# Reciprocal roots on GpSimd, gate steps on ScalarE, and fixed places for weight splits and the compression block in a two-layer hybrid trunk

## The chip, the cores and the metric

One core of one Trainium2 chip. The metric is the device time of the kernel in microseconds, one launch; of several runs the median is given.

## The reference

Two layers over one sequence of 256 tokens, width 1024, all in fp32. `D` is the width, `gate` a sigmoid of a small projection; the attention part is told in words.

```
for l in range(2):
    proj = rms_norm(h, norm_mix[l]) @ w_in[l]
    hq, hf, hi, hg, nq, kc, vc, ksl, vsl, ksw, vsw, ngate = split(proj)
    # HGRN2, 4 heads of 128, chunks of 64
    f = lb + (1 - lb) * sigmoid(hf);  k = 1 - f;  q = silu(hq)
    o_hg = rms_norm(gated_linear_recurrence(q, k, hi, log f)) * silu(hg)
    # NSA, 8 query heads of 64, 2 key/value heads
    kc, vc = compress(kc, ...), compress(vc, ...)   # silu(flat @ w1) @ w2
    o_nsa = gate * (compressed, selected and sliding-window attention),
            with q and all k normed (rms over 64) and rotated
    h = h + concat(o_hg, o_nsa) @ w_out[l]
    g, u = split(rms_norm(h, norm_ffn[l]) @ w_ffn_in[l])
    h = h + (silu(g) * u) @ w_ffn_out[l]
```

## The kernel before

Each fp32 product is made of three matmuls in a reduced format: `mm3` (L318 to L322) multiplies high parts with high parts, and each high part with the other low part. So each weight tile is split. Weights come in units of 128x1024 fp32 (512 KB): a DMA on the sync queue brings `wraw` (L122, four buffers), ScalarE copies it into the rounded `whi` (L142), and VectorE subtracts, `wlo = wraw - whi` (L143). Units are split five ahead of use, and six split units are held. Activations are split in the same way (`x`, L346 and L347).

The order on each engine is made by a scheduler from priorities; `after(a, b)` puts `a` behind `b` in that order without a semaphore of its own, and `products` is the list of all matmuls that `mm3` has issued, by which such places are named.

A layer runs: the norm and its transposition (`norm_T`, L324), the token projections B, C and A (`pt`), of which A gives the queries (`sq`, `qk_ss`, `qn`); the root `qk_rs` of the mean squares of queries and keys (`rstd`, L260 to L274); the gates of two heads (`gates(0)`, L376: `pf` for `hf`, `pq` for `hq`, two units each, 48 matmuls each); the compression block: `phid` (L505, 64 records, with the eight `w1` loads of 512 KB of L465), its copy `hid`, `phT` (L511), the SiLU (`hsg`, `hk`, `hv`), `pkc` (L522, L525), the compressed keys' root `kc_rs` and `kcb` (L544), `pkT` (L546). Then the scaled keys (`kraw`, L555, and `kA`, `kB`) and queries (`qn`, L570, and `qA`), `gates(1)`, the scores `pS`, the attention outputs, the recurrence (`pd`, `pl`, `po`, with the root `h_rs`), the output projection (`py`), the residual (L858), the feed-forward's norm with `norm_T`, the first feed-forward block by token tiles (`pgt`, `pgT`), and the feed-forward loop (`pgu`, `pz`).

`rstd` makes the reciprocal root on VectorE: a shift trick and three Newton steps, twelve operations. It is called four times in a layer: `qk_rs` (128x24), `kc_rs` (32x1) and `h_rs` (128x4, twice). `norm_T` makes its root already on GpSimd, by `pow` (L334, L335).

Around the feed-forward's norm the splits have places: the `wlo` of the first two feed-forward units stand behind the `x` subtractions of token tile 0, if they are made by then, and the `whi` of the next unit behind the last `x` copy:

```python
        last, lo = norm_T(0, gain1, *X2[:2], "b", hold=begin + HOLD[2])
        for hh in range(2):
            held = units[U["fu", 0, hh]][6]
            if held is not None:
                after(held, lo)
        state["behind"] = [last]
        residual(1, py, lo)
```

Of the kernel before, what the change touches and what calls it, by code (L numbers as in the profile page):

```python
# [89 lines left out]
def trunk(ctx: ExitStack, tc: tile.TileContext, x, w_in, w_out, lbl, gnorm, q_gain, k_gain,  # L90
# [23 lines left out]
    state = {"loaded": 0, "split": 0}  # L114

# [16 lines left out]
    def split_to(n):  # L132
        while state["split"] < min(n, len(units)):
# [7 lines left out]
            with tc.high_priority(offset=SPLIT_PRIO):  # L141
                after(S.activation(u[4], u[3], AF.Copy), state.pop("behind", ()))  # L142
                u[6] = V.tensor_sub(u[5], u[3], u[4].bitcast(F32))  # L143
            state["split"] += 1
# [115 lines left out]
    def rstd(ss, n, div, name, scr=None):  # L260
# [3 lines left out]
        a = sm.tile([128, 24], F32, name="rs_a")[:P, :n]  # L264
        b = sm.tile([128, 24], F32, name="rs_b")[:P, :n]
        y = sm.tile([128, 24], F32, name=name)[:P, :n]
        V.tensor_scalar(m, ss, 1.0 / div, EPS, op0=OP.mult, op1=OP.add)
        V.tensor_scalar(a.bitcast(I32), m.bitcast(I32), 1, None, op0=OP.logical_shift_right)
        V.tensor_scalar(y.bitcast(I32), a.bitcast(I32), -1.0, MAGIC, op0=OP.mult, op1=OP.add)
        for _ in range(3):  # L270
            V.tensor_mul(b, y, y)
            V.scalar_tensor_tensor(b, b, -0.5, m, op0=OP.mult, op1=OP.mult)
            V.scalar_tensor_tensor(y, b, 1.5, y, op0=OP.add, op1=OP.mult)
# [50 lines left out]
    def norm_T(t, gain, xh, xl, tag, behind=(), hold=None):  # L324

        with tc.high_priority():
            ss = sm.tile([128, 4], F32, name="n_ss")
            lo = []
# [7 lines left out]
            for c in range(2):  # L336
                cs = slice(512 * c, 512 * c + 512)
                V.scalar_tensor_tensor(xn[:, cs], h[:, t, cs], ss[:, 3:4], gain[c], op0=OP.mult, op1=OP.mult)
# [17 lines left out]
    for l in range(NL):  # L356
# [22 lines left out]
        def gates(hp):  # L379
# [6 lines left out]
            for i in range(2):  # L386
                hd = 2 * hp + i
                V.tensor_scalar(F[:, i], F[:, i], omlb[:, l, hd:hd + 1], lb[:, l, hd:hd + 1],
                                op0=OP.mult, op1=OP.add)
# [103 lines left out]
        rs = rstd(ss, 24, 64, "qk_rs")  # L493
        gates(0)
# [3 lines left out]
        for u in range(4):  # L498
            w = w1t[u]
            for jj in range(2):  # L500
                for kv in range(2):
                    for q in range(2):
                        j = 4 * u + 2 * jj + q
                        r0 = 64 * kv + 32 * q
                        PE.matmul(p[r0:r0 + 32], flat[:, kv, j], w[:, kv, 2 * jj + q],  # L505
                                  start=(j < 2), stop=(j >= 14))
# [3 lines left out]
        for c in range(2):  # L510
            PE.matmul(p[:, c], hid[:, 128 * c:128 * c + 128], C("sel"), start=True, stop=True)  # L511
# [225 lines left out]
        for t, p in proj_tok("hg"):  # L737
            V.tensor_copy(sgt[:, t], p)
# [114 lines left out]

        def residual(t, pp, behind=()):
            for a in range(2):
# [3 lines left out]
                after(r, behind[a:a + 1])  # L859

# [158 lines left out]
```

## Time and profile before

| | |
|---|---|
| time, median of 3 runs | 692.9 us (692.88 to 694.86) |
| the profiled execution | 694.62 us, its span 692.2 us |
| matmuls, TensorE | 4031, busy 98% of the span |
| VectorE, ScalarE, GpSimd busy | 69%, 55%, 3% |
| DMA | 118.92 MB, 172 GB/s in the mean |

In the rows, PE is TensorE, DVE VectorE, ACT ScalarE, POOL GpSimd, SP the sync engine whose queue issues the DMAs. A line such as L322 is that of the kernel before. A run of equal instructions is one row with its count. The time of a run of matmuls includes the end of the last one, which the next instruction overlaps; so the pace of a stretch is read from the starts. The idle time in square brackets is the engine's own, followed by what ended it.

### The profile page before, as it was taken

The page shows a single profiled execution, that of the slowest core. Times are in us where ns is not written, and L with a number is a line of the kernel's source. Part 1 is how long each engine was busy: PE and PEld are TensorE (multiplying, and loading weights), DVE is VectorE, ACT ScalarE, POOL GpSimd, SP SyncE. Part 2 cuts the span into 40 slices and gives each one's busy share as a digit, 9 for nine tenths or more (in the row PEclk, how much of TensorE's full clock was granted, in tenths as well). Part 3 has the DMA queues.
Part 4 walks back from the last instruction along what each step waited for, and adds up shares of the span by engine and source line. Part 5 has one row for each costly group of instructions (what it writes and reads, how often), then busy time and mean ns, then how long its engine had stood idle before and what let it go on. Part 6 is the DMA issues. An engine that isn't in the chain of part 4 may idle for free.

```text
span 692.2 us, 10682 instructions
## 1 busy us (share of the span) xinstructions
PE 674.9 (98%) x4031; PEld 567.5 (82%) x4031; DVE 477.8 (69%) x853; ACT 379.9 (55%) x676; POOL 23.1 (3%) x54
## 2 busy tenths in 40 slices
PE   5999999999999999999999999999999999999997
PEld 3869886688988888888878898768898888888886
DVE  4879997586765566665678979958676655666552
ACT  5446766665555555555456557747545555555540
POOL 1700000001000000000010000000000000000000
PEclk9999999999999999999999999999999999999999
DMA  7798521253865566656678632404366665665521
GB/s 242 237 346 261 171 64 59 91 165 105 266 196 183 182 189 195 194 184 190 180 237 293 203 119 63 122 1 124 122 199 204 195 194 186 188 197 191 183 90 61
DMA packets 86568, 118.92 MB, mean 172 GB/s; under 512 B 5035, under 2 KB 69365, under 8 KB 86518
## 3 DMA queue, kind: packets, MB, share of 16 engines
q1 hardware_dynamic: 86518, 118.26, 55.2%
q8 instruction: 31, 0.51, 0.3%
q14 instruction: 19, 0.16, 0.1%
HBM read 117.19 MB, written 1.05 MB: 171 GB/s over the span
## 4 chain that ended last, share of the span: by engine, by line
PE 82%; DVE 7%; DMA 4%; ACT 4%; issue 2%; POOL 1%; SPq 0%; POOLq 0%; DVEq 0%; ACTq 0%
PE pgu L905 20%; PE pz L322 17%; PE pt L322 12%; PE pgu L908 10%; PE py L322 6%; DVE wlo L143 3%; DMA wraw<-in_w_in_dram 3%; PE pl L766 2%; PE pO L667 2%; ACT whi L142 2%; PE pPT L657 2%; PE pf L322 1%; PE pxn L341 1%; DMA wraw<-in_w_ffn_in_dram 1%; PE pq L322 1%
## 5 line engine op out<-in xcount | busy, mean ns | idle before, releaser
L143 DVE TENSOR_TENSOR wlo<-wraw,whi 128x1024 fp32r<-128x1024 f32 (+1 forms) x204 | 245.3, 1206 | 146.9 <-ACT whi L142 145.8
L142 ACT ACTIVATE whi<-wraw 128x1024 fp32r<-128x1024 f32 (+1 forms) x204 | 212.2, 1043 | 154.7 <-PE pgu L905 42.5
L905 PE MATMUL pgu<-x,whi 128*128 128x512 f32 x640 | 174.8, 394 | 0.1
L905 PEld LDWEIGHTS pgu<-x,whi 128*128 128x128 f32 x640 | 110.6, 189 | 16.0 <-DVE ahl L946 0.3
L322 PE MATMUL pz<-whi,ahl 128*128 128x512 f32 x352 | 112.5, 391 | 0.0
L908 PEld LDWEIGHTS pgu<-x,wlo 128*128 128x128 f32 x640 | 98.1, 189 | 13.5
L908 PE MATMUL pgu<-x,wlo 128*128 128x256 f32 x640 | 101.7, 281 | 0.0
L322 PE MATMUL pt<-whi,x 128*128 128x512 f32 (+1 forms) x320 | 100.0, 386 | 0.0
L322 PEld LDWEIGHTS pz<-whi,ahl 128*128 128x128 f32 x352 | 65.9, 188 | 13.9 <-DVE ahl L922 0.5
L322 PE MATMUL pz<-wlo,ahl 128*128 128x512 f32 x176 | 68.9, 392 | 0.0
L322 PEld LDWEIGHTS pt<-whi,x 128*128 128x128 f32 x320 | 57.5, 190 | 8.3 <-DVE x L347 0.5
L322 PE MATMUL pt<-wlo,x 128*128 128x512 f32 (+1 forms) x160 | 62.0, 388 | 0.6 <-DVE wlo L143 0.6
L322 PE MATMUL py<-whi,x 128*128 128x512 f32 x128 | 41.8, 397 | 0.0
L322 PEld LDWEIGHTS pz<-wlo,ahl 128*128 128x128 f32 x176 | 33.0, 188 | 6.4
L322 PEld LDWEIGHTS pt<-wlo,x 128*128 128x128 f32 x160 | 30.5, 191 | 5.3 <-DVE wlo L143 1.5
L587 ACT ACTIVATE P<-pS,nm 128x128 f32<-128x128 f32 (+1 forms) x64 | 26.0, 426 | 6.7 <-DVE nm L634 5.4
L322 PEld LDWEIGHTS py<-whi,x 128*128 128x128 f32 x128 | 24.1, 188 | 4.8
L914 ACT ACTIVATE sl<-sl 128x512 f32<-128x512 f32 x20 | 12.7, 633 | 27.3 <-DVE sl L913 27.3
L766 PEld LDWEIGHTS pl<-Q,K 128*128 128x128 f32 x160 | 23.7, 191 | 3.3 <-issue 0.8
L322 PE MATMUL py<-wlo,x 128*128 128x512 f32 x64 | 25.0, 390 | 0.0
L322 PE MATMUL pf<-x,whi 128*128 128x256 f32 x128 | 23.8, 286 | 0.0
L322 PE MATMUL pgt<-whi,x 128*128 128x256 f32 x128 | 23.8, 285 | 0.0
(220 smaller groups left out, 862.4 us busy)
## 6 DMA issues: line engine op xcount, KB each, us to landing
wraw<-in_w_ffn_in_dram SPq DMA_DIRECT2D x88, 512.0 KB, 3.6
wraw<-in_w_in_dram SPq DMA_DIRECT2D x48, 512.0 KB, 5.0
wraw<-in_w_ffn_out_dram SPq DMA_DIRECT2D x44, 512.0 KB, 3.5
w<-in_cmp_w_k_dram SPq DMA_DIRECT2D x8, 512.0 KB, 5.1
w<-in_cmp_w_v_dram SPq DMA_DIRECT2D x8, 512.0 KB, 7.3
wraw<-in_w_out_dram SPq DMA_DIRECT2D x16, 256.0 KB, 4.0
wraw<-in_w_out_dram SPq DMA_DIRECT2D x8, 512.0 KB, 3.9
wraw<-in_w_in_dram SPq DMA_DIRECT2D x8, 280.0 KB, 5.4
```

Of the source, the lines that this page charges most:

```text
L142: after(S.activation(u[4], u[3], AF.Copy), state.pop("behind", ()))
L143: u[6] = V.tensor_sub(u[5], u[3], u[4].bitcast(F32))
L322: products.append(PE.matmul(o, a[u], b[v], start=start and i == 0, stop=stop and i == 2, skip_group_check=skip))
L341: tr = PE.transpose(p[:, 128 * k:128 * k + 128], xn[:, 512 * c + 128 * k:512 * c + 128 * k + 128], ident)
L587: e = S.activation(o, i, f, **kw)
L657: PE.transpose(p[:, 128 * hg:128 * hg + 128], P[t, g][:, hg, b, 128 * sb:128 * sb + 128], ident)
L667: m = PE.matmul(po[64 * g:64 * g + 64], vtok[:, b, sb, 64 * g:64 * g + 64], pts[g][0], start=(b == 0 and sb == 0), stop=False, skip_group_ ...
L766: m = PE.matmul(p[:, t0 + 64 * i:t0 + 64 * i + 64], K[:, i, ts], QF[:, i, ts].rearrange("p (n c a) -> p n c a", c=2, a=half)[:, :, 1], sta ...
L905: products.append(PE.matmul(pp[b], w[0][:, k, s], X[2][:, 4 * hh + k].rearrange("p c t -> p (c t)"), start=(hh == 0 and k == 0), stop=Fals ...
L908: products.append(PE.matmul(pp[b][:, T:], w[1][:, k, s], X[0][:, 4 * hh + k], start=False, stop=(hh == 1 and k == 3), skip_group_check=True))
L914: S.activation(sl, sl, AF.Silu)
```

## The change

It has five parts. (1) `rstd` makes the root on GpSimd, one affine step and one `pow`. (2) The affine step of the gates, `F*omlb + lb` (L388, twice for each pair of heads), goes from VectorE to ScalarE, and (3) so does the copy of the `hg` projection (L738). (4) In the compression block the `phid` matmuls are placed behind the 48th product since `gates(0)` began, and the `phT` matmuls behind the 62nd. (5) The norm's first half is a function of its own, `normed`, which returns the last square and the last `xn`; both norms of the feed-forward are begun ahead of the first block. Two lists, `hi_behind` and `lo_behind`, give the units of the feed-forward that follow their places: the `wlo` of the first stands behind the last `xn` of tile 0, of the second behind the last residual of tile 1, the `whi` of the third behind the last `x` copy of tile 0 and its `wlo` behind the last `xn` of tile 1, and the `whi` of the fourth behind the last square of tile 1.

```diff
--- before.py
+++ after.py
@@ -112,6 +112,7 @@
         return len(units) - 1
 
     state = {"loaded": 0, "split": 0}
+    hi_behind, lo_behind = [], []
 
     def load_to(n):
         while state["loaded"] < min(n, len(units)):
@@ -139,8 +140,9 @@
             u[4] = hi[:, : a * b].rearrange("p (a b) -> p a b", b=b)
             u[5] = lo[:, : a * b].rearrange("p (a b) -> p a b", b=b)
             with tc.high_priority(offset=SPLIT_PRIO):
-                after(S.activation(u[4], u[3], AF.Copy), state.pop("behind", ()))
+                after(S.activation(u[4], u[3], AF.Copy), hi_behind.pop(0) if hi_behind else ())
                 u[6] = V.tensor_sub(u[5], u[3], u[4].bitcast(F32))
+                after(u[6], lo_behind.pop(0) if lo_behind else ())
             state["split"] += 1
 
     def weights(i):
@@ -257,20 +259,13 @@
     for g in range(2):
         nc.gpsimd.memset(kB[64 - 64 * g:128 - 64 * g, g].bitcast(F32), 0.0)
 
-    def rstd(ss, n, div, name, scr=None):
+    def rstd(ss, n, div, name):
 
         P = ss.shape[0]
         m = sm.tile([128, 24], F32, name="rs_m")[:P, :n]
-        a = sm.tile([128, 24], F32, name="rs_a")[:P, :n]
-        b = sm.tile([128, 24], F32, name="rs_b")[:P, :n]
         y = sm.tile([128, 24], F32, name=name)[:P, :n]
-        V.tensor_scalar(m, ss, 1.0 / div, EPS, op0=OP.mult, op1=OP.add)
-        V.tensor_scalar(a.bitcast(I32), m.bitcast(I32), 1, None, op0=OP.logical_shift_right)
-        V.tensor_scalar(y.bitcast(I32), a.bitcast(I32), -1.0, MAGIC, op0=OP.mult, op1=OP.add)
-        for _ in range(3):
-            V.tensor_mul(b, y, y)
-            V.scalar_tensor_tensor(b, b, -0.5, m, op0=OP.mult, op1=OP.mult)
-            V.scalar_tensor_tensor(y, b, 1.5, y, op0=OP.add, op1=OP.mult)
+        nc.gpsimd.tensor_scalar(m, ss, 1.0 / div, EPS, op0=OP.mult, op1=OP.add)
+        nc.gpsimd.tensor_tensor(y, m, mhalf[:P].to_broadcast([P, n]), op=OP.pow)
         return y
 
     def setup_late():
@@ -321,11 +316,10 @@
         for i, (u, v) in enumerate(((0, 0), (0, 1), (1, 0))):
             products.append(PE.matmul(o, a[u], b[v], start=start and i == 0, stop=stop and i == 2, skip_group_check=skip))
 
-    def norm_T(t, gain, xh, xl, tag, behind=(), hold=None):
+    def normed(t, gain, behind=()):
 
         with tc.high_priority():
             ss = sm.tile([128, 4], F32, name="n_ss")
-            lo = []
             xn = wk.tile([128, D], F32, name="xn", tag="vs", bufs=2)
             for a in range(2):
                 cs = slice(512 * a, 512 * a + 512)
@@ -335,7 +329,16 @@
             nc.gpsimd.tensor_tensor(ss[:, 3:4], ss[:, 2:3], mhalf, op=OP.pow)
             for c in range(2):
                 cs = slice(512 * c, 512 * c + 512)
-                V.scalar_tensor_tensor(xn[:, cs], h[:, t, cs], ss[:, 3:4], gain[c], op0=OP.mult, op1=OP.mult)
+                m = V.scalar_tensor_tensor(xn[:, cs], h[:, t, cs], ss[:, 3:4], gain[c], op0=OP.mult, op1=OP.mult)
+        return xn, sq, m
+
+    def norm_T(t, gain, xh, xl, tag, behind=(), hold=None, xn=None):
+
+        if xn is None:
+            xn = normed(t, gain, behind)[0]
+        lo = []
+        with tc.high_priority():
+            for c in range(2):
                 p = bank("pxn", tag)
                 for k in range(4):
                     tr = PE.transpose(p[:, 128 * k:128 * k + 128], xn[:, 512 * c + 128 * k:512 * c + 128 * k + 128], ident)
@@ -385,8 +388,7 @@
             S.activation(F, pf.rearrange("p (h t) -> p h t", t=T), AF.Sigmoid)
             for i in range(2):
                 hd = 2 * hp + i
-                V.tensor_scalar(F[:, i], F[:, i], omlb[:, l, hd:hd + 1], lb[:, l, hd:hd + 1],
-                                op0=OP.mult, op1=OP.add)
+                S.activation(F[:, i], F[:, i], AF.Identity, scale=omlb[:, l, hd:hd + 1], bias=lb[:, l, hd:hd + 1])
             S.activation(K, F, AF.Copy, bias=1.0, scale=-1.0)
             pq = bank("pq", "a")
             proj_feat(("hq", hp), pq)
@@ -491,6 +493,7 @@
                              sn[:, None, None, s0].to_broadcast([128, 2, 4, 32]))
             V.tensor_add(dst, dst, qt)
         rs = rstd(ss, 24, 64, "qk_rs")
+        begin = len(products)
         gates(0)
 
 
@@ -502,13 +505,15 @@
                     for q in range(2):
                         j = 4 * u + 2 * jj + q
                         r0 = 64 * kv + 32 * q
-                        PE.matmul(p[r0:r0 + 32], flat[:, kv, j], w[:, kv, 2 * jj + q],
-                                  start=(j < 2), stop=(j >= 14))
+                        m = PE.matmul(p[r0:r0 + 32], flat[:, kv, j], w[:, kv, 2 * jj + q],
+                                      start=(j < 2), stop=(j >= 14))
+                        after(m, [products[begin + 47]])
         hid = wk.tile([128, 256], F32, name="hid", tag="qt", bufs=1)
         S.activation(hid, p, AF.Copy)
         p = bank("phT", "c")[:, :128].rearrange("p (c n) -> p c n", n=64)
         for c in range(2):
-            PE.matmul(p[:, c], hid[:, 128 * c:128 * c + 128], C("sel"), start=True, stop=True)
+            m = PE.matmul(p[:, c], hid[:, 128 * c:128 * c + 128], C("sel"), start=True, stop=True)
+            after(m, [products[begin + 61]])
         sg = wk.tile([128, 2, 64], F32, name="hsg")
         last_sig.append(S.activation(sg, p, AF.Sigmoid))
         hk = wk.tile([128, 2, 4, 32], F32, name="hk")
@@ -735,7 +740,7 @@
             S.activation(vh[:, t], p, AF.Copy)
         sgt = wk.tile([128, NT, 512], F32, name="sgt", tag="vs", bufs=2)
         for t, p in proj_tok("hg"):
-            V.tensor_copy(sgt[:, t], p)
+            S.activation(sgt[:, t], p, AF.Copy)
         si = S.activation(sgt, sgt, AF.Silu)
         after(si, exp_list[-4:])
         with tc.high_priority(offset=LEV_PRIO):
@@ -851,12 +856,15 @@
                 mm3(py[t][a], (mixT[0][:, kk, ts], mixT[1][:, kk, ts]), (w[0][:, 0, cs], w[1][:, 0, cs]),
                     kk == 4, kk == 3)
 
+        res = []
+
         def residual(t, pp, behind=()):
             for a in range(2):
                 cs = slice(512 * a, 512 * a + 512)
                 with tc.high_priority():
                     r = V.tensor_add(h[:, t, cs], pp[t][a], h[:, t, cs])
                 after(r, behind[a:a + 1])
+                res.append(r)
 
         for u in (4, 5):
             weights(U["wo", u])
@@ -877,13 +885,15 @@
         begin = len(products)
         for u in range(4):
             wo_part(1, u)
-        last, lo = norm_T(0, gain1, *X2[:2], "b", hold=begin + HOLD[2])
-        for hh in range(2):
-            held = units[U["fu", 0, hh]][6]
-            if held is not None:
-                after(held, lo)
-        state["behind"] = [last]
+        xn0, _, turn0 = normed(0, gain1)
+        last, lo = norm_T(0, gain1, *X2[:2], "b", hold=begin + HOLD[2], xn=xn0)
         residual(1, py, lo)
+        xn1, sq1, turn1 = normed(1, gain1)
+
+        for hh, ins in enumerate((turn0, res[-1])):
+            after(units[U["fu", 0, hh]][6], [ins])
+        hi_behind += [[last], [sq1]]
+        lo_behind += [[turn1]]
 
 
         X = X2
@@ -955,7 +965,7 @@
 
         begin = len(products)
         ffn_in_tok(0, 0)
-        norm_T(1, gain1, *X2[:2], "b", hold=begin + HOLD[3])
+        norm_T(1, gain1, *X2[:2], "b", hold=begin + HOLD[3], xn=xn1)
         ffn_in_tok(0, 1)
         py = [[bank("pz", "ab"[t]) for _ in range(2)] for t in range(NT)]
         late = []
```

The order on TensorE in layer 0, from the end of the query projection (`pt`) on; `phid`, `phT` and the first gates matmuls (`pf`), before:

```order
L322 MATMUL pt<-whi,x_128 128x512
L505 MATMUL phid<-w_355,flat 32x256 x8
L505 MATMUL phid<-w_358,flat 32x256 x8
L505 MATMUL phid<-w_361,flat 32x256 x8
L505 MATMUL phid<-w_364,flat 32x256 x8
L322 MATMUL pf<-x_128,whi 128x256 x2
L511 MATMUL phT<-cst,hid 128x64 x2
L322 MATMUL pf<-x_128,wlo 128x256
```

And now, some sixty rows later, at the end of `pq`; `pf` here is that of `gates(1)`:

```order
L317 MATMUL pq<-x_128,whi 128x256 x2
L317 MATMUL pq<-x_128,wlo 128x256
L508 MATMUL phid<-w_355,flat 32x256 x8
L508 MATMUL phid<-w_358,flat 32x256 x8
L508 MATMUL phid<-w_361,flat 32x256 x8
L508 MATMUL phid<-w_364,flat 32x256 x8
L317 MATMUL pf<-x_128,whi 128x256 x2
L317 MATMUL pf<-x_128,wlo 128x256
L317 MATMUL pf<-x_128,whi 128x256
L515 MATMUL phT<-cst,hid 128x64 x2
L317 MATMUL pf<-x_128,whi 128x256
L317 MATMUL pf<-x_128,wlo 128x256
```

The 64 `phid` matmuls (eight to a row) stood between `pt` and `pf` and now stand behind `pq`, so `pf` follows `pt` directly.

VectorE in layer 0, from the last mean squares (`qk_ss`) to the first split of a gates unit (`wlo`), before:

```order
L483 TENSOR_REDUCE qk_ss<-sq 128x2x4
L487 TENSOR_TENSOR qn<-pt,tabs 128x2x4x64
L490 TENSOR_TENSOR qt<-pt,tabs 128x8x32 x2
L267 TENSOR_SCALAR rs_m<-qk_ss 128x24
L492 TENSOR_TENSOR qn<-qn,qt 128x2x4x64
L268 TENSOR_SCALAR rs_a<-rs_m 128x24
L269 TENSOR_SCALAR qk_rs<-rs_a 128x24
L271 TENSOR_TENSOR rs_b<-qk_rs 128x24
L272 SCALAR_TENSOR_TENSOR rs_b<-rs_b,rs_m 128x24
L143 TENSOR_TENSOR wlo<-wraw,whi 128x1024
L273 SCALAR_TENSOR_TENSOR qk_rs<-rs_b,qk_rs 128x24
L271 TENSOR_TENSOR rs_b<-qk_rs 128x24
```

And now (L144 is the split, L560 and L575 the scalings that were L555 and L570):

```order
L485 TENSOR_REDUCE qk_ss<-sq 128x2x4
L489 TENSOR_TENSOR qn<-pt,tabs 128x2x4x64
L492 TENSOR_TENSOR qt<-pt,tabs 128x8x32 x2
L560 TENSOR_TENSOR kraw<-kraw,qk_rs 128x512
L494 TENSOR_TENSOR qn<-qn,qt 128x2x4x64
L575 TENSOR_TENSOR qn<-qn,qk_rs 128x512
L144 TENSOR_TENSOR wlo<-wraw,whi 128x1024
L575 TENSOR_TENSOR qn<-qn,qk_rs 128x512
L144 TENSOR_TENSOR wlo<-wraw,whi 128x1024 x6
```

The root's small operations are gone, and the scalings by `qk_rs` of the keys and of the first queries stand ahead of the first `wlo`.

VectorE around the feed-forward's norm of layer 0, from the residual of token tile 0 on (`xn` is the normed tile, `x_1633` its transposed low part), before:

```order
L858 TENSOR_TENSOR h<-py,h 128x512 x2
L338 SCALAR_TENSOR_TENSOR xn<-h,n_ss,gain 128x512 x2
L347 TENSOR_TENSOR x_1633<-pxn,x_1633 128x4x128 x2
L858 TENSOR_TENSOR h<-py,h 128x512 x2
L143 TENSOR_TENSOR wlo<-wraw,whi 128x1024 x2
L338 SCALAR_TENSOR_TENSOR xn<-h,n_ss,gain 128x512 x2
L143 TENSOR_TENSOR wlo<-wraw,whi 128x1024
L347 TENSOR_TENSOR x_1633<-pxn,x_1633 128x4x128 x2
L143 TENSOR_TENSOR wlo<-wraw,whi 128x1024
L941 TENSOR_TENSOR slt<-slt,pgt 128x256
```

And now (`x_1585` is that low part):

```order
L865 TENSOR_TENSOR h<-py,h 128x512 x2
L332 SCALAR_TENSOR_TENSOR xn<-h,n_ss,gain 128x512 x2
L144 TENSOR_TENSOR wlo<-wraw,whi 128x1024
L350 TENSOR_TENSOR x_1585<-pxn,x_1585 128x4x128 x2
L865 TENSOR_TENSOR h<-py,h 128x512 x2
L144 TENSOR_TENSOR wlo<-wraw,whi 128x1024
L332 SCALAR_TENSOR_TENSOR xn<-h,n_ss,gain 128x512 x2
L144 TENSOR_TENSOR wlo<-wraw,whi 128x1024 x2
L350 TENSOR_TENSOR x_1585<-pxn,x_1585 128x4x128 x2
L951 TENSOR_TENSOR slt<-slt,pgt 128x256
```

One `wlo` comes ahead of the first `x` subtractions, one between the residual and `xn` of tile 1, and two, for one, between that `xn` and the `x` subtractions of tile 1.

## Rows read from the trace of the kernel before

**Rows 1.** The page's first part: busy time, share of the span, instructions.

```profile
PE 674.9 (98%) x4031; PEld 567.5 (82%) x4031; DVE 477.8 (69%) x853; ACT 379.9 (55%) x676; POOL 23.1 (3%) x54
```

**Rows 2.** Waits of PE: who waits <- releaser: us, times, longest.

```profile
PE pxn L341 <- DVE xn L338: 7.7, 5, 5.8
```

**Rows 3.** Timeline, layer 0, PE: start, us, instruction, [idle before <-releaser].

```profile
46.63 3.66 PE L505 MATMUL phid<-w,flat 128*32 128x256 f32 x64
...
50.28 0.50 PE L322 MATMUL pf<-x,whi 128*128 128x256 f32 x2
...
50.80 0.66 PE L511 MATMUL phT<-cst,hid 128*128 128x64 f32 x4
...
51.97 0.39 PE L322 MATMUL pf<-x,wlo 128*128 128x256 f32 x1 [0.52 <-DVE wlo L143]
```

**Rows 4.** Timeline, the same stretch, ACT.

```profile
46.74 0.60 ACT L482 ACTIVATE sq<-pt 128x512 f32<-128x512 f32 x1 [4.78 <-PE pt L322]
...
49.16 1.06 ACT L142 ACTIVATE whi<-wraw 128x1024 fp32r<-128x1024 f32 x1 [1.83 <-DMA wraw<-in_w_in_dram]
```

**Rows 5.** Timeline, SP's DMA queue (issues, then units), same stretch.

```profile
38.78 1.42 SPq L465 DMA_DIRECT2D w<-in_cmp_w_v_dram  x1
40.29 32.93 SPq L122 DMA_DIRECT2D wraw<-in_w_in_dram  x16
```

**Rows 6.** Timeline, the same stretch, DVE.

```profile
47.37 0.69 DVE L483 TENSOR_REDUCE qk_ss<-sq 128x8 f32<-128x512 f32 x1 [2.70 <-ACT sq L482]
...
50.70 1.22 DVE L143 TENSOR_TENSOR wlo<-wraw,whi 128x1024 fp32r<-128x1024 f32 x1
...
59.06 0.69 DVE L555 TENSOR_TENSOR kraw<-kraw,qk_rs 128x512 f32<-128x512 f32 x1
```

**Rows 7.** Timeline, POOL: tables at the start, feed-forward's norm of layer 0.

```profile
24.24 0.85 POOL L310 TENSOR_SCALAR tabs<-tabs 128x256 f32<-128x256 f32 x1
...
161.43 0.31 POOL L334 TENSOR_SCALAR n_ss<-n_ss 128x1 f32<-128x1 f32 x1 [70.45 <-ACT xn L332]
...
161.82 0.57 POOL L335 TENSOR_TENSOR n_ss<-n_ss,mhalf 128x1 f32<-128x1 f32 x1
...
168.67 1.12 POOL L334 TENSOR_SCALAR n_ss<-n_ss 128x1 f32<-128x1 f32 x1 [6.28 <-ACT xn L332]
```

**Rows 8.** Groups by line and shape, DVE: busy us, mean ns, idle before.

```profile
L388 DVE TENSOR_SCALAR F<-F,omlb,lb 128x256 f32<-128x256 f32 x8 | 3.2, 405 | 0.3 <-ACT F L385 0.3
...
L271 DVE TENSOR_TENSOR rs_b<-h_rs 128x4 f32<-128x4 f32 x12 | 1.9, 162 | 0.3
```

**Rows 9.** Timeline, PE: the waits in the middle of the kernel.

```profile
74.67 0.24 PE L546 MATMUL pkT<-cst,kcb 32*128 32x32 f32 x1 [0.45 <-DVE kcb L544]
...
79.84 0.39 PE L617 MATMUL pS<-cab,idb 128*128 128x512 bf16 x1 [0.43 <-DVE kB L566]
...
171.35 0.63 PE L341 MATMUL pxn<-cst,xn 128*128 128x128 f32 x4 [0.73 <-DVE xn L338]
...
419.44 1.16 PE L751 MATMUL pd<-Q,K 128*128 128x128 f32 x8 [0.46 <-DVE Q L396]
```

**Rows 10.** PE at start, then windows at end (seventh value after times: granted clock).

```profile
14.65 1.05 PE L322 MATMUL pt<-whi,x 128*128 128x512 f32 x2
...
15.51 0.53 PE L322 MATMUL pt<-wlo,x 128*128 128x512 f32 x1
...
16.58 0.62 PE L322 MATMUL pt<-whi,x 128*128 128x512 f32 x2
...
17.03 0.40 PE L322 MATMUL pt<-wlo,x 128*128 128x512 f32 x1
...
690.00:691.60 1.60, 0.00 (x0) 0.00 (x0) 0.00 (x0) 0.00 (x0) 0.00 (x0) 1.00 0.14 47
...
691.60:692.20 0.60, 0.00 (x0) 0.00 (x0) 0.00 (x0) 0.00 (x0) 0.00 (x0) 0.53 0.00 0
```

**Rows 11.** Timeline, PE in the feed-forward's norm of layer 0.

```profile
172.40 0.48 PE L322 MATMUL pgt<-whi,x 128*128 128x256 f32 x2
```

## What the change is predicted to do

> **What bounds the kernel now.** The share of busy time says TensorE: 98% of the span, against 69% for VectorE, 55% for ScalarE and 3% for GpSimd [rows 1]. So work taken from VectorE is worth something only where TensorE waits for VectorE. The view of waits on TensorE lists them: 7.7 us for the transposed norm (`pxn`), of which 5.8 are one wait at the very start [rows 2]. In mid-kernel the timelines leave small gaps: `pkT` 0.45, `pS` 0.43, `pxn` 0.73 and `pd` 0.46 us [rows 9]. Measured against the pace of the matmuls around each they cost 0.61, 0.61, 0.89 and 0.62 us; `pxn` comes again in layer 1 (0.88) and `pd` once more. With some smaller ones, all that VectorE makes TensorE wait in mid-kernel is near 6 us. That is the ceiling of what a lighter VectorE can bring, however much leaves it.
>
> What is taken off VectorE is much more: 96 small root operations at 0.16 us, some 15 us, and the eight affine steps, 3.2 us [rows 8], with four copies. None of it is worth its length.
>
> One stretch matters more than these: the end of the NSA projection of layer 0. TensorE finishes `pt` at 46.6, does the 64 `phid` matmuls in 3.66 us, two `pf` matmuls and the four `phT`, and the first `pf` matmul that needs a `wlo` starts at 51.97 after a wait of only 0.52 [rows 3]. The reason for that wait stands on other engines. ScalarE idles 1.83 us for the first gates unit and starts its `whi` at 49.16 [rows 4]; that unit was issued at 40.29 on the sync queue, behind the eight `w1` loads [rows 5]; `wlo` follows on VectorE at 50.70 [rows 6]. In this stretch, then, the weights bound the work, and `phid`, whose own weights are there, is what TensorE does while it waits.
>
> **The change part by part.**
>
> *`phid` and `phT` behind the gates.* The DMA order in layer 0 stays as it is, but TensorE now comes to `pf` at 46.63 and has nothing else. Before, the span from 46.63 to 51.97 contained 3.66 us of `phid` and 0.66 of `phT`; the last result of a run overlaps the next instruction by about 0.2 each, so some 3.9 us of real work. This work now comes after `pq`. If the first `wlo` matmul starts at W, the loss is (W − 51.97) + 3.9.
>
> W follows from VectorE's new order. After the last `qk_ss` reduction (47.37 plus 0.69, 48.06 [rows 6]) GpSimd makes the root; VectorE does three rotary products meanwhile, but then stands at `kraw`, which needs the root, and the add to `qn`, the `qn` scaling and the `wlo` stand behind it. So a wait is added in front of the first gates weight. The root is two POOL operations. For a 128x1 tile they take 0.31 and 0.57 us [rows 7]; the new one is 128x24 and no row shows that. The affine step I take at 0.36. The power is bounded below by 0.57 plus little: a 128x256 POOL operation of the cheap kind takes 0.85 [rows 7], 0.54 more than the 128x1 one, so 23 more elements add 0.05: 0.63. From above: let each element cost as much as the power costs more than the affine step at one element, 0.57 − 0.31 = 0.26, so 23 × 0.26 more, 6.6. I take 1.9, nearer the lower end, because both rows of one element are mostly start-up. Then the root is ready at 48.06 + 0.36 + 1.9 + 0.2 for two handovers = 50.5; three operations of some 0.65 (0.69 as shown [rows 6], ends overlapping) end at 52.4; the `wlo` of 1.22 ends at 53.6. The loss is 53.6 − 52.0 + 3.9 = **5.5 us**. With the power at 0.63, the root is there at 49.2, the `wlo` starts at 51.2 and ends at 52.4: 4.3. With 6.6 it ends at 58.3: 10.2. Even if no root stood there, `whi` ends at 50.22 and the `wlo` at 51.5: 3.4. So a loss of this step is nearly certain; the layer-1 order already had `phid` late, and nothing is lost there.
>
> A word on the lock between VectorE and GpSimd. The first affine step of the feed-forward's norm takes 0.31 us, and the second, beside two `wlo` subtractions, 1.12 [rows 7]. In the Trainium skill, "SBUF — State Buffer", section "SBUF: two separate sides", VectorE and GpSimd share a port pair that is locked for a whole instruction, so that the loser is fully blocked; that speaks against roots on GpSimd. The longer of the two rows agrees with it. By that rule each of the two POOL operations could wait for one VectorE operation more, some 0.7 us here, and the sum would be about 5.4 instead of 4.7. By the row alone, the operations beside this root read from PSUM, unlike `wlo`, and I add nothing.
>
> *Roots elsewhere, gates, copy.* `kc_rs` sat on the chain to `pkT`: ten of twelve small operations go, two POOL operations come; and `pkT` is behind fewer matmuls. I take 0.5 of its 0.61 back. `kB` is no longer behind twelve operations, its 0.6 goes. Against these, ScalarE gets eight affine steps of about 0.4 and four copies of about 0.6 (the square of the same shape is 0.60 [rows 4]); half idle, it hides them, except where it evicts scores beside the gates, for which I take 0.5 back as a loss. Together −0.6. `h_rs` feeds `poT`, for which TensorE does not wait: 0; without that cover it would cost the 0.6 to 1.9 of a power.
>
> *The feed-forward's norm.* The `wlo` of the two first units now have places behind the last `xn` of tile 0 and the last residual of tile 1. This removes the pair of `wlo` ahead of `xn` of tile 1, and `pxn` comes earlier, so its 0.89 [rows 9] goes. But two `wlo` (1.22 each, [rows 6]) now stand between that `xn` and the `x` subtraction, which only one did before. TensorE has 20 `pgt` matmuls ahead of `pgT` there, not 30, and it waits at the first `pgt` of tile 1 that needs that part of `x`, some 13 matmuls behind those at 172.40 [rows 11], by about as much. I take 0 per layer, bounds −0.9 and +0.3.
>
> *Layer 1.* `pkT` comes earlier, some −0.2; `pd` keeps its gap.
>
> Sum: 5.5 − 0.6 + 0 − 0.2 = **+4.7 us**. The profiled execution took 694.62 us, 1.7 over the median of 692.9; the same addition to the median gives **697.6 us** (699.3 for the profiled one's own).
>
> **The rivals.** *The other side: the relief is worth more than the bubble.* If all gaps in mid-kernel went (6.0) and the first gates unit came by 46.6, ahead of some `w1` loads, the loss would shrink to the root's wait alone, about 1.5 to 3.4: 692.9 − 6.0 + 3.4 = 690.3. It decides when the bubble is below the recovered gaps. For it: the gaps all end on VectorE. Against it: the unit's DMA stands unchanged behind the `w1` loads and the queue was full there [rows 5]. Chance 0.06.
>
> *Cheap power, norm gaps gone.* 4.3 for the bubble, −1.1 for `pkT` and `pS`, −0.9 in each norm, −0.2: +1.2, 694.1, no difference that a measurement tells. Chance 0.20.
>
> *The clock falls in the bubble.* After the last matmul near 688 the granted clock is 1.00 until 691.6 and then 0.53 [rows 10], the lower of its two levels, 1.2 GHz. The new bubble at 46.6 is 3.5 to 6 us long with two matmuls in it, and may end in that state. At the low level a matmul of `pt` took 0.43 us by the starts at 14.65 and 15.51, against 0.23 by those at 16.58 and 17.03 [rows 10], so the pace falls to about half; if that lasts 4 us, as long as the bubble before it, 2 us of work are lost: 699.6. The Trainium skill, "TensorE: Matmul & The Clock Gate", Part 1, says that the gate sets the rate by how busy the engine has recently been; the rows of the end agree. Chance 0.25.
>
> *A dear power.* With the upper bound the loss is 10.2 and the sum +9.4: 702.3. Chance 0.07.
>
> *The change does not do what it says:* the order shows that it does, apart from `phid` standing behind `pq` too and not only behind `pf`; no chance of its own.
>
> **How the numbers follow.** The forecast itself has 0.42, the cases 0.06, 0.20, 0.25 and 0.07. About 0.3%, 2.1 us, is what a measurement of this kernel can tell from no change. Faster by more than that: 0.06. Within: 0.20. Slower: 0.42 + 0.25 + 0.07 = 0.74. The range leaves out the first rival and the dear power: from 693.8 (the second rival with a little more recovered) to 701.5 (the fallen clock with the power near 3.8).
>
> **What would show it.** In the profile after: a gap on `pf` near 46.6, TensorE's first `wlo` matmul at about 53.6, ended by VectorE's `wlo` behind `kraw`; `phid` after `pq`; POOL's 128x24 power near 1.9 us; no wait at `pkT` and `pS`; in the norm no wait on `pxn` but one on `pgt`; all later times shifted by about 5 us. The prediction is wrong if `pf` starts before 50, if the gaps in the norms vanish with nothing in their place, or if VectorE's lighter load shortens stretches in which TensorE shows no gap.

## The result and the profile after

| | before | changed |
|---|---|---|
| median of 4 runs | 693.02 us (692.88 to 694.86) | 697.56 us (697.23 to 697.96) |
| ratio, 95% interval | | 1.006 (1.0042 to 1.0077) |
| profiled execution, its span | 694.62, 692.2 us | 697.69, 695.9 us |

The changed kernel is slower by 4.5 us; 697.6 was forecast. The sum came out, but two of its terms did not: they were far off in opposite directions.

TensorE's busy time did not change, 674.4 us against 674.9 [rows 1]; VectorE lost 16 us and POOL gained as many:

```profile
PE 674.4 (97%) x4031; PEld 569.6 (82%) x4031; DVE 462.0 (66%) x745; ACT 385.9 (55%) x688; POOL 39.4 (6%) x70
```

The waits on TensorE, changed kernel (who waits <- releaser: us in total, times, longest us):

```profile
PE pf L317 <- DVE wlo L144: 4.7, 1, 4.7
PE pxn L344 <- DVE xn L332: 4.6, 2, 4.4
PE pf L317 <- ACT whi L143: 3.6, 1, 3.6
PE pgain L251 <- DMA gain<-in_norm_mix_dram: 2.4, 1, 2.4
PE pgt L317 <- DVE x L350: 1.3, 2, 0.7
...
```

The wait of 3.6 us on `pf` for a `whi` is new, and the one for a `wlo` has grown from 0.52 [rows 3] to 4.7. Of the five `pxn` waits of before [rows 2] the one at the start and a small one stay, those in the norms are gone, and `pgt` waits in their place. The new hole in layer 0, TensorE's timeline (start, us, instruction, idle before and what ended it):

```profile
44.70 0.39 PE L317 MATMUL pt<-whi,x 128*128 128x512 f32 x1
48.71 0.74 PE L317 MATMUL pf<-x,whi 128*128 128x256 f32 x2 [3.63 <-ACT whi L143]
54.14 0.58 PE L317 MATMUL pf<-x,wlo 128*128 128x256 f32 x1 [4.69 <-DVE wlo L144]
54.52 0.63 PE L317 MATMUL pf<-x,whi 128*128 128x256 f32 x2
54.95 0.41 PE L317 MATMUL pf<-x,wlo 128*128 128x256 f32 x1
...
59.38 0.40 PE L317 MATMUL pf<-x,whi 128*128 128x256 f32 x2
59.62 0.29 PE L317 MATMUL pf<-x,wlo 128*128 128x256 f32 x1
```

VectorE in the same stretch:

```profile
45.75 0.69 DVE L485 TENSOR_REDUCE qk_ss<-sq 128x8 f32<-128x512 f32 x1 [2.71 <-ACT sq L484]
...
51.05 0.69 DVE L560 TENSOR_TENSOR kraw<-kraw,qk_rs 128x512 f32<-128x512 f32 x1 [3.36 <-POOL qk_rs L268]
...
52.87 1.22 DVE L144 TENSOR_TENSOR wlo<-wraw,whi 128x1024 fp32r<-128x1024 f32 x1
```

and POOL:

```profile
46.53 0.22 POOL L267 TENSOR_SCALAR rs_m<-qk_ss 128x24 f32<-128x24 f32 x1 [18.18 <-DVE qk_ss L485]
46.83 4.19 POOL L268 TENSOR_TENSOR qk_rs<-rs_m,mhalf 128x24 f32<-128x24 f32 x1
```

`kraw` waits 3.36 us for the power, and the `wlo` that ends TensorE's wait is the third operation behind it. Windows over the stretch (core 0: us, then busy us of PE, PEld, DVE, ACT, POOL, the granted clock, DMA share, GB/s):

```profile
45.10:48.70 3.60, 0.00 (x0) 0.00 (x0) 1.95 (x4) 1.65 (x2) 2.09 (x2) 1.00 1.10 348
49.00:54.10 5.10, 0.45 (x2) 0.16 (x1) 3.05 (x5) 3.17 (x3) 2.02 (x1) 0.50 0.35 113
54.10:59.10 5.00, 4.96 (x23) 4.96 (x24) 4.32 (x5) 1.06 (x1) 0.00 (x0) 0.51 0.74 204
59.10:62.00 2.90, 2.90 (x26) 2.90 (x26) 1.28 (x2) 1.06 (x1) 0.00 (x0) 1.00 1.04 326
```

The first of these windows has no matmul; behind it the clock is granted at half, 1.2 GHz, through the rest of the hole and 5 us of work: 0.215 us per matmul by the starts at 54.52 and 54.95, against 0.12 by those at 59.38 and 59.62.

Where the time went is seen from the starts of the same matmuls in both traces:

| start of | before | changed | difference | step |
|---|---|---|---|---|
| 65th `pt` | 30.67 | 29.39 | -1.28 | -1.28 |
| first `pf` that needs `wlo` | 51.97 | 54.14 | +2.17 | +3.45 |
| 48th `pf` | 57.45 | 61.78 | +4.33 | +2.16 |
| 48th `pq` | 63.21 | 67.54 | +4.33 | 0 |
| first `py` | 142.27 | 147.74 | +5.47 | +1.14 |
| first `pgu` (behind the norm) | 179.64 | 185.01 | +5.37 | -0.10 |
| first `pf` of layer 1 | 384.24 | 389.47 | +5.23 | -0.14 |
| first `po` of the second pair, layer 1 | 474.83 | 479.21 | +4.37 | -0.86 |
| first `pgu` of layer 1 | 514.80 | 519.05 | +4.25 | -0.12 |
| last `pz` | 687.59 | 691.46 | +3.87 | -0.38 |

The first step is not the change's: over the traces of all the kernels below the first `pxn` starts anywhere between 10.06 and 11.94 us. From the 65th `pt` on the changed kernel takes 5.15 us more. The step to `py` contains `phid` and `phT`, which were done before the hole until now. In the changed kernel they take 3.59 and 0.47 us from their first start to the start of what follows (67.75 to 71.34, 71.92 to 72.39), 4.06 together; so the rest of the attention became 2.92 us shorter.

One execution of those below, the profiled one of the run with parts 2 and 3 alone, took 2338.82 us, its matmuls several times as long as elsewhere; its time and its trace are left out.

### The profile page after: what moved, and what is told of

It reads as the page before. It is cut to its first block, busy times and chain, and to the rows that moved or that the text cites. A ratio compares the mean times of both kernels' runs of the same rounds, so it can differ in the third digit from the quotient of the medians.

```text
span 695.9 us, 10608 instructions
## 1 busy us (share of the span) xinstructions
PE 674.4 (97%) x4031; PEld 569.6 (82%) x4031; DVE 462.0 (66%) x745; ACT 385.9 (55%) x688; POOL 39.4 (6%) x70
## 4 chain that ended last, share of the span: by engine, by line
PE 88%; DVE 4%; ACT 2%; POOL 2%; DMA 2%; issue 2%; SPq 0%; POOLq 0%; DVEq 0%; ACTq 0%
PE pgu L915 21%; PE pz L317 17%; PE pt L317 12%; PE pgu L918 11%; PE py L317 5%; PE pf L317 4%; PE pq L317 3%; PE pl L771 2%; PE pO L672 2%; PE pgt L317 2%; PE pPT L662 2%; DMA wraw<-in_w_in_dram 2%; DVE wlo L144 1%; PE phid L508 1%; ACT xn L326 1%
## 5 line engine op out<-in xcount | busy, mean ns | idle before, releaser
L144 DVE TENSOR_TENSOR wlo<-wraw,whi 128x1024 fp32r<-128x1024 f32 (+1 forms) x204 | 245.1, 1206 | 151.5 <-ACT whi L143 150.7
L317 PE MATMUL pt<-whi,x 128*128 128x512 f32 (+1 forms) x320 | 103.7, 391 | 0.0
L317 PE MATMUL pf<-x,whi 128*128 128x256 f32 x128 | 26.6, 304 | 3.6 <-ACT whi L143 3.6
L771 PEld LDWEIGHTS pl<-Q,K 128*128 128x128 f32 x160 | 26.6, 190 | 4.0 <-issue 0.4
L317 PEld LDWEIGHTS pf<-x,whi 128*128 128x128 f32 x128 | 21.9, 208 | 4.9 <-ACT whi L143 4.0
```

Of the source, the lines that this page charges most:

```text
L317: products.append(PE.matmul(o, a[u], b[v], start=start and i == 0, stop=stop and i == 2, skip_group_check=skip))
L771: m = PE.matmul(p[:, t0 + 64 * i:t0 + 64 * i + 64], K[:, i, ts], QF[:, i, ts].rearrange("p (n c a) -> p n c a", c=2, a=half)[:, :, 1], sta ...
```

## The experiments

All ratios are against the kernel before on the same chip, whose medians there were 694.2 to 694.5 us. The theory: the loss is made of the uncovered `phid`, of what waits in VectorE's queue for POOL's power, and of TensorE's clock after the hole.

**Undoing one cause at a time.** First, `phid` and `phT` back at their old places:

```diff
-                        after(m, [products[begin + 47]])
...
-            after(m, [products[begin + 61]])
```

> The changed kernel without part 4: phid and phT go back between pt and pf. Theory: phid's 3.9 us fall into the hole that the root leaves, while wlo still waits for the 4.19 us power: 697.6 - 3.9 = 693.7, the hole from the end of phT to wlo still some 5 us. Whether the clock falls again decides up to 2.2 us: 693.7 if it falls, 691.5 if it holds. Rival, that the place of phid costs nothing since wlo bounds the stretch: 697.6.

Ratio 1.0024 (1.0012 to 1.0037), some 1.8 us over before: more than 693.7 would give (1.001). `phid` did fall into the hole, the clock fell too, and a new wait came. TensorE and ScalarE of this run:

```profile
54.11 0.71 PE L514 MATMUL phT<-cst,hid 128*128 128x64 f32 x4 [3.69 <-ACT hid L511]
```

```profile
53.68 0.38 ACT L511 ACTIVATE hid<-phid 128x256 f32<-128x256 f32 x1 [3.81 <-DVE qn L494]
```

`hid` shares the buffer `qt` with the rotary products; the add to `qn` that frees it stands behind `kraw`, and so behind the power. Everything that ScalarE had queued behind `hid`, the next `whi` too, waited with it.

Second, the root of queries and keys alone back on VectorE, with the twelve old operations as `rstd_v`:

```diff
-        rs = rstd(ss, 24, 64, "qk_rs")
+        rs = rstd_v(ss, 24, 64, "qk_rs")
```

> The changed kernel with qk_rs alone made by the twelve VectorE operations again; phid stays late. Theory: the first wlo comes 3.7 us earlier (no wait for the power): 697.6 - 3.7 = 693.9, with the hole some 5 us and two pf in it; if the clock then holds, 2.2 less, 691.7. Rival, that the power is hidden by other work: 697.6.

1.0012 (1.0001 to 1.0023), as the theory says with the fallen clock: the first `pf` with `wlo` starts at 51.64, the clock is at 0.50 from 51.6 to 57.6. So the power was not hidden.

**One part alone on the kernel before.** The late places of `phid` and `phT` (part 4):

```diff
+        begin = len(products)
...
+                        after(m, [products[begin + 47]])
...
+            after(m, [products[begin + 61]])
```

> The kernel before with part 4 alone. Theory: wlo at 51.97 as before, phid's 3.9 us no longer in the hole: 693.0 + 3.9 = 696.9, up to 2.2 more if the clock falls in a hole of 5 us: 699.1. Rival, that the late place pays by a shorter chain to pkT: 0.6 to 1.2 less, 695.7 to 696.3 without the clock.

1.0077 (1.006 to 1.0094), 5.4 us, within the theory's 3.9 to 6.1. The clock fell (1.63 us of lost pace), and the stretch from `pq` to `py`, without the 4.06 us of `phid` and `phT`, was 2.03 us shorter than before: the late place brings an order in the attention that is worth 2 us, with all roots still on VectorE. Some of it went again, at `pa` of layer 1, the transposition of the compression's inputs (1.2 us of wait).

All eight roots on POOL, nothing else (part 1; `rstd` as in the changed kernel):

> The kernel before with part 1 alone, all eight roots on POOL. Theory: first wlo 3.7 us later than before, hole of some 4.5 us behind phid: 693.0 + 3.7 = 696.7, up to 2.2 more with a fallen clock, and 1 to 3 less for small gaps that close on VectorE: 694 to 698. Rival, that the roots gain nothing elsewhere: 696.7 to 698.9.

1.0106 (1.0086 to 1.0126), 7.4 us: the worst of all, and over either bound. The later `wlo` cost 3.4 and the clock 1.8, as expected; but the stretch from `pq` to `py` grew by 2.28 us instead of shrinking, and a new wait of 1.4 us stood at `pgT`. The scheduler had put the small matmuls of the recurrence (`pl`), two by two, between the single transpositions of the attention (`pPT`). TensorE of this run, and then of the changed kernel:

```profile
131.17 0.33 PE L650 MATMUL pPT<-cst,P 128*128 128x128 f32 x1
131.43 0.25 PE L768 MATMUL pl<-Q,K 128*32 128x32 f32 x2
131.61 0.33 PE L650 MATMUL pPT<-cst,P 128*128 128x128 f32 x1
```

```profile
127.00 0.33 PE L780 MATMUL pl<-Q,K 128*32 128x32 f32 x16
127.26 0.50 PE L317 MATMUL pt<-whi,x 128*128 128x512 f32 x1
...
130.20 1.09 PE L662 MATMUL pPT<-cst,P 128*128 128x128 f32 x8
131.22 1.08 PE L672 MATMUL pO<-PT,vtok 128*64 128x512 f32 x4
```

A `pPT` and two `pl` alternating take 0.44 us a round. Eight `pPT` in a row take 1.02 us, 0.13 each, and sixteen such `pl` in a row 0.26 us, 0.02 each, so that the same work would be some 0.16 in rows of its own kind. No wait shows in these rows. `pl` and `pPT` follow each other directly 27 times between `pq` and `py` in this run, 4 times before and 3 times in the changed kernel; from each start to the next they take 18.1 us together in this run and 15.3 before. A wait of 1.0 us at `pd` in the same stretch took the place of those that before had at `pkT` and `pS`.

The affine steps and the copy on ScalarE, nothing else (parts 2 and 3):

```diff
-                V.tensor_scalar(F[:, i], F[:, i], omlb[:, l, hd:hd + 1], lb[:, l, hd:hd + 1],
-                                op0=OP.mult, op1=OP.add)
+                S.activation(F[:, i], F[:, i], AF.Identity, scale=omlb[:, l, hd:hd + 1], bias=lb[:, l, hd:hd + 1])
...
-            V.tensor_copy(sgt[:, t], p)
+            S.activation(sgt[:, t], p, AF.Copy)
```

> The kernel before with parts 2 and 3 alone: the gates' affine steps and the copy of the hg projection on ScalarE. Theory (VectorE was in nobody's way there except behind pd and pS): the stretch from the gates to the output projection shorter by 0 to 1 us in each layer, ratio 0.998. Rival, that these parts hold the recovery that the changed kernel shows in that stretch (2.9 us in layer 0, 0.9 in layer 1) and that the roots alone do not: ratio 0.9945.

1.0005 (0.9983 to 1.0028): no gain that can be told, and not the rival's 0.9945. Without a trace, only the time speaks. The same edit taken back from the changed kernel:

> The changed kernel with the affine steps and the copy back on VectorE. Theory: as the changed kernel within 1 us, ratio 1.006 to 1.0075. Rival, that ScalarE's share is what recovers: the 2.9 and 0.9 us come back as a loss, ratio 1.011.

1.0095 (1.0063 to 1.0127), between theory and rival. By the trace both stretches of attention are 1.0 us longer than in the changed kernel, and `pa` at the start of layer 1 waits 1.0 us for `kvc`. So these parts show no gain alone, and some 2 us beside POOL's roots, by the medians (1.0095 against 1.006); the intervals of the two ratios overlap, so it is the trace that carries this, and its execution was the slowest of four. The parts do not add.

**The clock.** Extra matmuls whose results nobody reads, 28 ahead of the first `pf` and 36 behind the second, each of `pf`'s size, in layer 0 of the changed kernel:

```diff
+            pz = bank("pfill", "e")
+            f1 = [PE.matmul(pz[:, :256], X[0][:, 0, 0:128], X[0][:, 0], start=True, stop=True) for _ in range(28)]
...
+            after(products[begin], [f1[-1]])
+            with tc.high_priority():
+                f2 = [PE.matmul(pz[:, :256], X[0][:, 0, 0:128], X[0][:, 0], start=True, stop=True) for _ in range(36)]
+            after(f2[0], [products[begin + 1]])
+            after(products[begin + 2], [f2[-1]])
```

> The changed kernel with 64 extra pf-sized matmuls of values that nobody reads, 28 ahead of the first pf and 36 behind the second, so TensorE is busy in most of the hole; all waits stay. It does 7.7 us of matmuls more than the changed kernel. Theory (the clock at half rate cost 2.2 us behind the hole): granted clock 1.00 throughout and 2.2 us less than the changed kernel, ratio to before 1.003. Rival, that the low clock delays nothing since the weights bound the stretch anyway: no gain, 1.006; more if the extra matmuls overrun the hole.

1.0027 (1.0013 to 1.004), as the theory says. Windows of this run:

```profile
45.00:49.00 4.00, 3.65 (x30) 3.41 (x29) 1.95 (x4) 1.66 (x2) 2.26 (x2) 1.00 1.10 348
49.00:54.20 5.20, 4.71 (x38) 4.51 (x38) 3.02 (x5) 3.18 (x3) 2.15 (x1) 1.00 0.27 84
54.30:60.00 5.70, 5.70 (x47) 5.70 (x48) 4.93 (x5) 1.06 (x1) 0.00 (x0) 1.00 0.79 228
```

The wait for `wlo` is where it was (`pf` at 54.27), the clock is 1.00 throughout, and the 48th `pf` comes 5.50 us after the third, as before (5.48), against 7.64 in the changed kernel. 7.7 us of useless work did not make the kernel slower but faster, 1.0027 against 1.006.

**Undoing the causes together.** In layer 0 `phid` ahead of `pf` again, with `phT` left at its late place, and the root of queries and keys on VectorE:

```diff
-                        after(m, [products[begin + 47]])
+                        if l > 0:
+                            after(m, [products[begin + 47]])
```

> As the run with qk_rs on VectorE, and in layer 0 phid also goes back ahead of pf, while phT stays at its late place. Theory (the loss is the uncovered phid, the late wlo and the fallen clock; the late phT keeps the better order in the attention): against the run with qk_rs on VectorE alone, 3.9 less for phid and 2 less for a clock that no longer falls, the hole being 1.5 us instead of 5: some 5 below the kernel before, ratio 0.993. Rival, that the gain in the attention came from the late phid itself and goes with it: 2 to 3 below, ratio 0.996.

0.9949 (0.9924 to 0.9973): faster than before, the clock at 1.00 where it had fallen. The interval holds theory and rival; by the trace some half of the gain in the attention went again (2.9 us less than before from the 65th `pt` on); `pkc` waits 0.6 us there. The same edit with the root on POOL:

> The changed kernel with phid alone put back ahead of pf in layer 0; root on POOL, phT late. Theory: against the changed kernel 3.9 less; the hole from the end of phid (about 3.5 after pt) to wlo stays some 5 us, so the clock falls still: ratio to before 1.001. If the clock holds: 0.998. Rival, that hid waits for its buffer and holds something else up, as it held phT in the first run: above 1.003.

1.0004 (0.9985 to 1.0023), as expected with a fallen clock (0.60 from 55.6 to 62.0). And this edit with the scalings by the root placed behind the second gates `wlo`, so that no weight waits for the power:

```diff
+        if l == 0:
+            after(m, [units[U["hf", 0, 1]][6]])
```

(once for `kraw`, once for each `qn`.)

> The changed kernel with phid ahead of pf in layer 0, phT late, and the scalings by qk_rs placed behind the second gates wlo, so that the root stays on POOL and no weight waits for it. Theory (the 4.19 us power hurts only by what is queued behind the scaling on VectorE): wlo starts when whi ends, W some 4 us earlier than in the changed kernel, hole 1.5 us, clock holds: as the run with the root on VectorE and phid early or better by what VectorE saves, ratio 0.992 to 0.993. Rival, that VectorE and POOL block each other and the power or the wlo stretches: wlo longer than 1.22 us beside the power, ratio 0.995 to 1.0.

0.9916 (0.9887 to 0.9945), 689.88 us. TensorE, VectorE and POOL of this run:

```profile
49.51 0.39 PE L317 MATMUL pf<-x,wlo 128*128 128x256 f32 x1 [0.76 <-DVE wlo L144]
```

```profile
48.22 1.23 DVE L144 TENSOR_TENSOR wlo<-wraw,whi 128x1024 fp32r<-128x1024 f32 x1 [0.22 <-ACT whi L143]
49.74 1.23 DVE L144 TENSOR_TENSOR wlo<-wraw,whi 128x1024 fp32r<-128x1024 f32 x1 [0.29 <-ACT whi L143]
50.88 0.69 DVE L561 TENSOR_TENSOR kraw<-kraw,qk_rs 128x512 f32<-128x512 f32 x1
```

```profile
46.41 4.20 POOL L268 TENSOR_TENSOR qk_rs<-rs_m,mhalf 128x24 f32<-128x24 f32 x1
```

The power takes as long as ever, and nothing waits for it here: two `wlo` run beside it, and `kraw` starts behind them without a pause. A root on POOL was not the fault; what stood behind it was.

**Two further steps, not shown to bring more.** The `wlo` of the third feed-forward unit behind the `x` subtractions of tile 1:

```diff
-        lo_behind += [[turn1]]
...
+        third = units[U["fu", 0, 1] + 1][6]
+        _, lo = norm_T(1, gain1, *X2[:2], "b", hold=begin + HOLD[3], xn=xn1)
+        after(third, lo)
```

> The run with the scalings behind the wlo, and the wlo of the third feed-forward unit behind the x subtractions of token tile 1 instead of behind xn. Theory (the 0.8 us at pgt is nothing but the wlo subtractions that stand between xn and x): 0.8 less in each layer, 1.6 in all, no wait at pgt, ratio 0.9893. Rival, that the third wlo then comes too late for its matmuls: a new wait at pgu of about one wlo, ratio 0.9916 or above.

0.9941 (0.9919 to 0.9964). The wait at `pgt` is gone, 0.83 us in each layer by the starts, as the theory says. The forecast ratio of 0.9893 was missed even so, since as much was lost elsewhere, above all at `pkc`, which waits 1.6 us in this run against 0.5 in the one before it, with the same instructions in the same order: the ScalarE copies ahead of it waited for their weights, as one row of this run shows:

```profile
63.44 1.06 ACT L143 ACTIVATE whi<-wraw 128x1024 fp32r<-128x1024 f32 x1 [0.50 <-DMA wraw<-in_w_in_dram]
```

And with `phT` early too:

> The same, and in layer 0 phT also at its place behind the first pf matmuls. Theory (hid is no longer held by the rotation's buffer, since qn's add now stands ahead of wlo): phT falls into the hole that is left, 0.5 less, and the 0.66 at pkc goes: ratio 0.9877. Rival, that phT waits for hid there as in the first run: above 0.9893; or that the order in the attention gets worse by as much as is saved: 0.9893.

0.9933 (0.9911 to 0.9954), 689.2 us, against 0.9877 expected; the wait at `pkc` is gone, one of 0.7 at `pd` has come. From the 65th `pt` to the last `pz` this run took 651.8 us, the one before it 654.6, that with the scalings moved 653.2 and the kernel before 656.9. The three intervals overlap: all three beat both kernels, and which is best stays open.

## Why the prediction was right, and where it was not

**The hole (forecast +5.5).** The mechanism was right in each link: `pf` followed `pt` with nothing between and waited, its `wlo` stood behind `kraw`, `kraw` waited for the root, and `phid` and `phT` were no longer there to cover it. The mis-sized term is the power: 1.9 us were taken, between 0.63 and 6.6; it took 4.19. POOL's groups by shape in the changed kernel show how it grows:

```profile
L268 POOL TENSOR_TENSOR qk_rs<-rs_m,mhalf 128x24 f32<-128x24 f32 x2 | 8.4, 4186 | 0.2
...
L329 POOL TENSOR_TENSOR n_ss<-n_ss,mhalf 128x1 f32<-128x1 f32 x8 | 4.5, 569 | 0.7
```

(4186 - 569) / 23 is 157 ns for each further column. The reasoning that a 128x1 row is mostly start-up was wrong: the upper bound's way of counting, by column, was right, with a smaller price than the 0.26 taken. The first `pf` that needs a `wlo` came 3.45 us later, and `phid` and `phT` cost 4.06: 7.5 instead of 5.5. With the root on VectorE that `pf` came no later than before (51.64 against 51.97, the 65th `pt` at 30.39 against 30.67), so the 3.45 are the root's. The first run shows the 3.69 us that `phT` waits for the same root, by way of `hid`. The lock between VectorE and POOL, for which the forecast added nothing, cost nothing at this root: the affine step took 0.22 us, and the power was as long in layer 1 beside a `wlo` (4.18) as in layer 0 without one (4.19).

**The clock (a rival with 0.25, some 2 us).** It happened, and cost 2.16 us; the run with the filled hole shows it by itself. It was worked out as a case apart from the forecast, but both came together, in the very hole that the forecast described. In the forecast's sum this term was missing. With the power and the clock both as they came, the prediction's own sum gives 7.8 for the hole, 2 for the clock and -0.8, so +9.0 and 701.9 us, which lies outside its range.

**What comes back (forecast -0.8).** It was 2.92 in the attention of layer 0, 0.86 in that of layer 1, 0.14 and 0.38 in and behind the feed-forward loops: 4.3 without the norms. `pkT` and `pS` of layer 0 lost their gaps as forecast, and `pd` of layer 1, which was to keep its gap, loses 0.19 instead of 0.62 against its pace. Of the 2.92, the gaps are 1.0: between the 48th `pq` and the first `py` TensorE was idle for 1.06 us before and for 0.02 now. The rest has no wait in before to go back to, so counting waits could not find it. It lies in the order in which the scheduler interleaves small matmuls: from each start to the next, the 128 `pl` take 7.90 us instead of 9.52 and the 40 `pO` (the attention outputs) 7.77 instead of 9.44, while `pt` and `pf` take 1.3 more. One place shows it, TensorE of the kernel before and then of the changed one:

```profile
133.39 0.33 PE L775 MATMUL pl<-Q,K 128*64 128x64 f32 x4
133.65 0.49 PE L679 MATMUL pO<-pcT_sb,vblk 128*128 128x128 f32 x2
134.07 0.33 PE L775 MATMUL pl<-Q,K 128*64 128x64 f32 x2
...
135.00 0.71 PE L679 MATMUL pO<-pcT_sb,vblk 128*128 128x128 f32 x4
135.55 1.06 PE L806 MATMUL p<-Q,K 128*128 128x128 f32 x8
```

```profile
135.13 1.16 PE L684 MATMUL pO<-pcT_sb,vblk 128*128 128x128 f32 x8
...
138.31 0.45 PE L780 MATMUL pl<-Q,K 128*64 128x64 f32 x8
```

Before, these eight `pO` and eight `pl` alternate and take 2.16 us (133.39 to 135.55); now each kind stands together, and they take 0.91 and 0.38 (to the starts of what follows, 136.04 and 138.69). Which part of the change brings this order stays open: the late `phid` alone gave 2.0 with the roots on VectorE, the roots alone took 2.28, 2.14 of the 2.92 stay with `phid` and `phT` at their old places (the first run), and the ScalarE parts gave nothing that can be told alone and about 1 in each attention with the roots on POOL.

**The norm (forecast 0 per layer).** -0.10 and -0.12. The exchange was the one described, VectorE and then TensorE of the changed kernel:

```profile
176.17 2.36 DVE L144 TENSOR_TENSOR wlo<-wraw,whi 128x1024 fp32r<-128x1024 f32 x2
178.44 1.28 DVE L350 TENSOR_TENSOR x<-pxn,x 128x512 fp32r<-128x512 f32 x2
```

```profile
179.18 0.51 PE L317 MATMUL pgt<-whi,x 128*128 128x256 f32 x2 [0.66 <-DVE x L350]
```

The gap at `pxn` of [rows 9] went (0.89), and one at `pgt` came (0.82). The run with the third `wlo` later shows that it is the pair of `wlo` that makes it.

**The sum.** 7.5 + 2.2 - 4.3 - 0.2 is 5.2, by the trace 5.15; 4.5 by the medians. That the forecast of 4.7 met it was luck: a hole and a clock worth 4.2 more than forecast stood against 3.7 more of recovery. Of the signs that the prediction named against itself, one came: stretches in which TensorE shows no gap became shorter. They did so by their order: the late `phid` alone gained 2.0 us, 1.5 of them where no gap had been, with VectorE's work unchanged, and the roots alone, with VectorE lighter, lost 2.28. Another, `pf` before 50, came only in name: it starts at 48.71, but the last `pt` is 1.61 us earlier too (44.70 against 46.31). The rival of the other side asked for a unit that came earlier; the runs reached its sign in another way, by moving what waits.

## What to carry to other kernels

Before moving work to an idle engine, look at what stands behind the first reader of its result: here nothing waited for the power's 4.19 us once the scaling stood behind the weights' splits, and the kernel took some 6 us more when it stood ahead (0.9916 against 1.0004, part of it the clock). Work that seems to be on the path may be what covers a wait and keeps TensorE's clock up; move it only with something to put in its place. When a scheduler sets the order, a part measured alone can be worth nothing and still help beside another, as ScalarE's parts do by the trace (no gain alone, 1.0 us in each attention beside POOL's roots), so run the parts apart and together.

## What was not expected of the hardware

The power on POOL took 0.57 us for one column and 4.19 for 24, 0.157 for each further one; by that four columns would take 1.04, and they took 1.02.

A VectorE subtraction held up a power that began just behind it, but not one that was already running. POOL and VectorE of the changed kernel at the two `h_rs` of layer 0, and then at `qk_rs` of layer 1:

```profile
148.63 1.02 POOL L268 TENSOR_TENSOR h_rs<-rs_m,mhalf 128x4 f32<-128x4 f32 x1
...
151.93 2.04 POOL L268 TENSOR_TENSOR h_rs<-rs_m,mhalf 128x4 f32<-128x4 f32 x1
...
393.13 4.18 POOL L268 TENSOR_TENSOR qk_rs<-rs_m,mhalf 128x24 f32<-128x24 f32 x1
```

```profile
151.87 1.23 DVE L144 TENSOR_TENSOR wlo<-wraw,whi 128x1024 fp32r<-128x1024 f32 x1 [0.31 <-ACT whi L143]
...
393.58 1.22 DVE L144 TENSOR_TENSOR wlo<-wraw,whi 128x1024 fp32r<-128x1024 f32 x1
```

The second `h_rs`, begun 0.06 us behind a `wlo`, is 1.02 us longer than the first. In layer 1 the `wlo` began 0.45 us behind the power, and both kept their lengths, 1.22 and 4.18; in the run with the scalings moved the power had run for 1.8 us when the `wlo` began, and both kept theirs, 4.20 and 1.23. In the Trainium skill, "SBUF — State Buffer", section "SBUF: two separate sides", a GpSimd operation that reads SBUF and a VectorE operation with two SBUF inputs, as `wlo` is, share a port pair: whichever starts first holds it for its whole instruction, and the other is blocked. The second `h_rs` agrees; the two `qk_rs`, beside which a `wlo` should have been blocked, do not.

Alternating small matmuls of two shapes costs TensorE time in which no wait is seen: 0.44 us for a round of `pPT` and two `pl`, against some 0.16 for the same three among their like.
